# A table of expert products stored in blocks of two experts by two tokens instead of row by row

## The chip, the cores and the metric

The kernel runs on one core of a Trainium2 chip. The metric is the device time of one execution in microseconds (us); the time before is the median of three runs. A core has a matrix engine (PE, whose weight loads are listed as PEld), a vector engine (DVE), an activation engine (ACT), a general engine (POOL) and a queue engine (SP), which run side by side, each through its own instructions in order, and wait for each other by semaphores. Matrix products land in PSUM, all other tiles lie in SBUF; both have 128 partitions.

## The reference

The reference is one layer of a streaming encoder on 256 tokens of width 2048: a mixing block (gated MLP and retention) and then PEER, a lookup into 16384 experts. The change is in PEER. Expert number `n1 * 128 + n2` has a row of `emb_u` and a row of `emb_v`. For each token, 8 heads pick 16 experts each, 128 picks in all:

```python
    q = (hf @ wq).reshape(t_, PEER_HEADS, 2, PEER_DHALF)
    sc = jnp.einsum('thpd,hpnd->thpn', q, subkeys)
    v1, i1 = lax.top_k(sc[:, :, 0], PEER_TOPK)
    v2, i2 = lax.top_k(sc[:, :, 1], PEER_TOPK)
    cand = (v1[..., :, None] + v2[..., None, :]).reshape(t_, PEER_HEADS, ...)
    cidx = (i1[..., :, None] * PEER_NKEYS + i2[..., None, :]).reshape(...)
    top, sel = lax.top_k(cand, PEER_TOPK)
    eidx = jnp.take_along_axis(cidx, sel, axis=-1)
    gate = jax.nn.softmax(top, axis=-1)
    u = emb_u[it]
    a = jnp.einsum('td,thkd->thk', xt, u)
    w = jax.nn.gelu(a, approximate=False) * gt
    vv = emb_v[it]
    return jnp.einsum('thk,thkd->td', w, vv)
```

## The kernel before, in words

The kernel computes the PEER sums mostly as dense products over all experts, and only a slice of the columns by gathering rows. It goes through these stages:

- up to about 1119 us, the mixing block, the queries and the routing (`route_post`), which leaves for each token and pick the two halves `i1`, `i2` of the expert's number and the gate;
- 1119 to 1600 us, the u-products. For each value `n` of `i1`, PE multiplies the 128 experts of that block (columns 768 to 2047 of `emb_u`) with all 256 tokens. The results of two values of `i1` come to one PSUM bank, and line 926 copies it into `A`. `A` has 128 partitions (the `i2` of an expert) and 128 x 256 floats in each: by `i1`, then by token. It is 128 KB a partition. The other 768 columns are done by gathered rows (line 757) and dot products on DVE (line 764);
- 1600 to 1806 us, pick and scatter. The tokens go through in 32 units of 8 (`SET`). `one_hot` writes for each token a 128x128 matrix that has a one where the column's number is the pick's `i2` (`o2`, lines 960 and 961 on ACT or 957 on DVE, some tokens on POOL at line 963) or its `i1` (`o1`). `turned` transposes `o2` on PE (line 974, PSUM tile `pb`) and copies the result on ACT (line 975, `oh2T`). `pick` (line 984) multiplies it with all 128 values of `A` that belong to one token, so that each of the token's 128 picks gets the row of its `i2` (PSUM tile `pk`); line 988 on DVE takes from that row the value at its `i1`. `weight` adds the gathered part and makes the weight of each pick with GELU and the gate (lines 993 to 995). `scatter` multiplies `o1` by the weights on POOL (line 1000), PE sums them by expert (line 1004, PSUM tile `pw`), and ACT writes the 128x128 weights of four tokens back over the products in `A` (line 1005, the *put*);
- 1808 to 2327 us, the v-products. For each value `i` of `i1`, `v_load` takes the row `A[:, i]` of 256 token weights, splits it in a rounded part `wh` (line 1085, ACT) and a rest `wl` (line 1087, DVE), splits a block of `emb_v` likewise (lines 1089 and 1091), and PE sums the three products over all 128 blocks (line 1141). Gathered rows of `emb_v` (line 757) are weighed and added on DVE (line 1073) four gathers late. The end adds the residual and normalises.

In `A` of before, the values of one token are 256 floats (1024 bytes) apart, the values of one `i1` lie side by side. So line 926 writes side by side, line 984 reads with steps of 1024 bytes, line 1005 writes with steps of 1024 bytes (it goes through its source in order, token by token), and lines 1085 and 1087 read side by side.

The order of the work is written out by loops: in iteration `u` of the stage come `pick(u)`, `weight(u)`, the one-hot and the transposes of unit `u + 1`, `scatter(u - 2)`, and the one-hot `o1` of unit `u`. A scheduler then fixes one order for each engine. The PSUM tiles have 2 (`pb`), 3 (`pk`) and 3 (`pw`) buffers, the one-hots 3 (`o1`) and 5 (`o2`), the turned ones 4.

Of the kernel before, what the change touches and what calls it, by code (L numbers as in the profile page):

```python
# [10 lines left out]
F32 = mybir.dt.float32  # L11
# [5 lines left out]
ALU = mybir.AluOpType  # L17
# [5 lines left out]
P = 128  # L23
T = 256
# [9 lines left out]
NK = 128  # L34
# [82 lines left out]
def block_kernel(ctx, tc, a, out):  # L117
    nc = tc.nc
    def pool(name, side, bufs=1, space=None):
        stack = ExitStack()  # L120
        kw = {} if space == bass.MemoryType.DRAM else {"reuse_waits": "tile"}
        if space is not None:
            kw["space"] = space
        return stack.enter_context(tc.tile_pool(name=name, bufs=bufs, side=side, **kw)), stack
# [642 lines left out]
    def dot(tt, n, early=False, after=None):  # L767
        if early:
            g = gather(late["pg"], "eg", u_rows, UG, EG, tt, n)
        else:  # L770
            g = gather(ph, "hT", u_rows, UG, 8, tt, n, after)
        times(g, tt, n)
# [102 lines left out]
    def columns():  # L875
        softmax()
        nc.scalar.copy(idr, ident)
        for dst, src in ((i1T, i12[:, 0]), (i2T, i12[:, 1]), (gT, gate)):
            pt = bank("pt")
            for tt in range(TT):  # L880
                nc.tensor.transpose(pt[:, tt * P:(tt + 1) * P], src[:, tt], ident)
            nc.scalar.copy(dst, pt[:, :T])
            if dst is i2T:
                nc.scalar.mul(neg, pt[:, :T], -1.0)
# [4 lines left out]
    sums = {}  # L889

    def u_products(n):
        for m in range(n + len(ready), min(n + 2, 2 * NK)):
            ready.append(u_load(m))
        hi, lo = ready.pop(0)
        first, last = n % 2 == 0, n % 2 == 1
        if n % 4 == 0:
            sums[n // 4] = bank("mmu").rearrange("p (b t) -> p b t", b=2) if n // 4 % 2 else pm.tile([P, 2, T], F32, tag="mm", name="mmu")
        acc = sums[n // 4][:, n // 2 % 2]
        k0, k1 = HALF[n % 2]
        steps = ((hi, 0), (hi, 1), (lo, 0)) if n >= DIRECT else ((hi, None),)  # L900
        for i, (w, part) in enumerate(steps):
            for k in range(k0, k1):
                x = late["x1T"][:, UK + k] if part is None else h2T.op(part, UK + k)
                mm = nc.tensor.matmul(acc, w[:, k - k0], x, start=(first and k == 0 and i == 0),  # L904
                                      stop=(last and k == FK - 1 and i == len(steps) - 1))
        return mm

    for n in range(DIRECT):
        mm = u_products(n)
    late["pg_s"].close()  # L910
    st_s.close()
    big, big_s = pool("big", "left")
    A = big.tile([P, NK, T], F32, tag="big", name="A")
    pick_room, pick_room_s = pool("pickroom", "left")
    colT = pick_room.tile([P, 4, T], F32, name="colT")
    i1T, i2T, wT, gT = (colT[:, i] for i in range(4))
# [5 lines left out]
    for n in range(2 * NK):  # L922
        if n >= DIRECT:
            mm = u_products(n)
        if n % 4 == 3:
            nc.scalar.copy(A[:, n // 2 - 1:n // 2 + 1], sums.pop(n // 4))
        if n == COLS:
            columns()
        while done < rate * (n + 1 - PRE):
            dot(*todo.pop(0), after=mm)  # L930
            done += 1
# [10 lines left out]
    def psum(tag, bufs):  # L942
        b = pq.tile([P, 512], F32, tag=tag, bufs=bufs, name=tag)
        return b, b.rearrange("p (t n) -> p t n", t=4)
# [33 lines left out]
    def pick(u):  # L978
        for h in range(2):
            t0 = u * SET + 4 * h  # L980
            oh = ohs.pop((u, h))
            pk, pkv = psum("pk", 3)
            for t in range(4):
                mm = nc.tensor.matmul(pkv[:, t], oh[:, t], A[:, :, t0 + t], start=True, stop=True)
                tc.declare_no_dep(mm.ins, group="scattered", reason="other tokens' columns")
            for t in range(4):
                jk = p2.tile([P, P], F32, tag="jk", bufs=2, name="jk")
                nc.vector.scalar_tensor_tensor(jk, iota, i1T[:, t0 + t:t0 + t + 1], pkv[:, t],
                                               op0=ALU.is_equal, op1=ALU.mult, accum_out=wT[:, t0 + t:t0 + t + 1])
# [7 lines left out]
    def scatter(u):  # L997
        t0 = u * SET
        o1, o2 = o1s.pop(u), o2s.pop(u)
        nc.gpsimd.tensor_tensor(o1, o1, wT[:, t0:t0 + SET, None].to_broadcast([P, SET, P]), op=ALU.mult)  # L1000
        for h in range(0, SET, 4):
            pw, pwv = psum("pw", 3)
            for t in range(4):
                nc.tensor.matmul(pwv[:, t], o2[:, h + t].bitcast(F32), o1[:, h + t], start=True, stop=True)  # L1004
            put = nc.scalar.copy(A[:, :, t0 + h:t0 + h + 4].rearrange("p n t -> p t n"), pwv)
            tc.add_to_no_dep_group("scattered", put.ins)

    units = T // SET
# [18 lines left out]
    for u in range(-LEAD, units + LAG):  # L1027
        if 0 <= u < units and u % half == 0:
            tt = u // half
            while tt and fetched:  # L1030
                last_dot()
            pt, _ = psum("pk", 3)
            nc.tensor.transpose(pt[:, :P], wrow[:, tt], ident)
            nc.vector.tensor_copy(agT[:, tt * P:(tt + 1) * P], pt[:, :P])
        if 0 <= u < units:
            pick(u)
            weight(u)
        if u + LEAD < units:
            o2s[u + LEAD] = one_hot(1, u + LEAD, (ON2 if u * SET < T // 2 else ON3)[u % 4])
            turned(u + LEAD)  # L1040
        if 0 <= u < half and fetched and (u + 1) * LEFT > took * half:
            last_dot()
        if u >= LAG:
            scatter(u - LAG)
        if 0 <= u + 1 - LAG + AHEAD1 < units:
            v = u + 1 - LAG + AHEAD1
            o1s[v] = one_hot(0, v, ON1[v % 4])
        if 0 <= u < units and u % half == half - 1:
            pt, _ = psum("pk", 3)
            nc.tensor.transpose(pt[:, :P], wT[:, tt * P:(tt + 1) * P], ident)  # L1050
            nc.vector.tensor_copy(wrow[:, tt], pt[:, :P])
    W = A

    p2_s.close()
    pq_s.close()
    pick_room_s.close()
# [23 lines left out]
    def v_load(i):  # L1080
        room, bufs = (p3, 1) if i % 3 == 2 else (pv, 2)
        vb = room.tile([P, GV], F32, tag="vb", bufs=bufs, name="vb")
        nc.sync.dma_start(vb, v_cols[i * P:(i + 1) * P])
        wh = p3.tile([P, T], F32R, tag="wh", bufs=3, name="wh")
        nc.scalar.copy(wh, W[:, i])  # L1085
        wl = p3.tile([P, T], F32R, tag="wl", bufs=3, name="wl")
        nc.vector.tensor_tensor(wl, W[:, i], wh.bitcast(F32), op=ALU.subtract)  # L1087
        vh = p3.tile([P, GV], F32R, tag="vh", bufs=2, name="vh")
        nc.scalar.copy(vh, vb)  # L1089
        vl = p3.tile([P, GV], F32R, tag="vl", bufs=2, name="vl")  # L1090
        late["split"] = nc.vector.tensor_tensor(vl, vb, vh.bitcast(F32), op=ALU.subtract)  # L1091
        return vh, vl, wh, wl

    spent = A.rearrange("p n t -> p (n t)")
    x1 = spent[:, :TT * D].rearrange("p (t d) -> p t d", t=TT)
    xo = spent[:, TT * D:2 * TT * D].rearrange("p (t d) -> p t d", t=TT)
    ga2, gf = spent[:, 4 * D:5 * D], spent[:, 5 * D:6 * D]
# [39 lines left out]
    def product(i, ops, j, tt, n):  # L1137
        vh, vl, wh, wl = ops
        l, r = ((wh, vh), (wl, vh), (wh, vl))[j]
        c, w = chunks[n]  # L1140
        return nc.tensor.matmul(yp[tt][n][:, :w], l[:, tt * P:(tt + 1) * P], r[:, c:c + w],  # L1141
                                start=(i == 0 and j == 0), stop=(i == NK - 1 and j == 2))

    nxt = v_load(0)
    nc.scalar.sqrt(rf, late["ssum"])  # L1145
    done, rate = 0, len(todo) / (NK - ENDS)
    for i in range(NK - 2):
        ops = nxt
        nxt = v_load(i + 1)
        for j in range(3):  # L1150
            for tt in range(TT):
                for n in range(len(chunks)):
                    mm = product(i, ops, j, tt, n)
        while todo and done < rate * (i + 1):
            fly(*todo.pop(0), after=mm)
            done += 1
        while len(flying) > BEHIND:
            weigh()
        if i == BACK:
            restore(mm)  # L1160
    ends = [nxt, v_load(NK - 1)]
    while flying:
        weigh()
# [64 lines left out]
```

## Time and profile before

| what | value |
| --- | --- |
| median of three runs | 2359.65 us (2357.73, 2359.65, 2369.08) |
| the profiled execution | 2363.87 us |
| its span, first to last instruction | 2362.1 us |
| PE busy | 2199.1 us, 93% |
| DVE busy | 1779.2 us, 75% |
| ACT busy | 1028.9 us, 44% |
| POOL busy | 938.0 us, 40% |
| mean granted clock of PE | 0.978 |

Busy time is that of the whole span; the stages have different limits, and the shares of one stage are read from windows. A busy PE is one that has products under way, which overlap; the time from the start of one group of products to the start of the next tells what a group takes.

### The profile page before, as it was taken

Reading aid. Unit: us, or ns where it says so; the run is one execution under the profiler, and the core shown is the slowest. Engines: PE = TensorE matmul, PEld = TensorE weight load, DVE = VectorE, ACT = ScalarE, POOL = GpSimd, SP = SyncE. Lnnn points to the kernel's source line nnn. Section 1 sums busy time; section 2 is a strip of 40 time slices with the busy share of each in tenths; the row PEclk is TensorE's granted clock in tenths of the full one; section 3 lists DMA queues with packets and bytes.
Section 4 is the critical chain, followed back from the end, with each engine's and each line's share of the span. In section 5 each row is a group of like instructions: output and inputs, shape, how many; then the busy total and the mean of one; then the engine's idle time right before and its main releaser. Section 6 shows DMA issues by size and latency. Waiting matters only on the chain. (4 is left out here: it accounts for less than half of the span.)

```text
span 2362.1 us, 37306 instructions
## 1 busy us (share of the span) xinstructions
PE 2199.1 (93%) x13988; PEld 1953.3 (83%) x13988; DVE 1779.2 (75%) x3416; ACT 1028.9 (44%) x1439; POOL 938.0 (40%) x750
## 2 busy tenths in 40 slices
PE   6899999999999998983999999998999999999996
PEld 3577778999999888883899899898998878778885
DVE  3469878888888755788677767668766878888887
ACT  3245555643344344100344444447875444344433
POOL 0000000000000001766344444348776887887884
PEclk9999999999999999996999999999999999999998
DMA  9987778778877864767899899893103999999997
GB/s 352 370 308 270 276 276 290 267 285 291 289 280 291 286 209 166 275 203 228 292 307 312 303 309 312 294 310 102 54 1 112 327 331 318 323 333 331 340 323 265
DMA packets 144313, 638.27 MB, mean 270 GB/s; under 512 B 20721, under 2 KB 26625, under 8 KB 112001
## 3 DMA queue, kind: packets, MB, share of 16 engines
q1 hardware_dynamic: 102146, 459.65, 54.7%
q0 software_dynamic: 41984, 176.23, 21.7%
q8 instruction: 110, 1.80, 0.3%
q14 instruction: 73, 0.60, 0.1%
HBM read 631.59 MB, written 4.20 MB: 269 GB/s over the span
## 5 line engine op out<-in xcount | busy, mean ns | idle before, releaser
L757 POOL DMA_INDIRECT gat<-in_peer_v_rows,eidx x256 | 417.3, 1630 | 106.6 <-issue 40.2
L757 POOL DMA_INDIRECT gat<-in_peer_u_rows,eidx x256 | 313.0, 1223 | 309.8 <-DVE ulo L712 149.1
L213 ACT CAST whi<-wt 128x2048 fp32r<-128x2048 f32 x130 | 248.1, 1908 | 290.7 <-PE mm L414 222.8
L764 DVE SCALAR_TENSOR_TENSOR gat<-gat,h2b 128x768 f32<-128x768 f32 x256 | 245.2, 960 | 151.0 <-DMA gat<-in_peer_u_rows,eidx 147.9
L904 PE MATMUL mmu<-h2T,uhi 128*128 128x256 f32 x2360 | 325.8, 285 | 33.9 <-ACT uhi L711 33.9
L215 DVE TENSOR_TENSOR wlo<-wt,whi 128x2048 fp32r<-128x2048 f32 (+1 forms) x130 | 292.3, 2249 | 54.9 <-ACT whi L213 51.0
L904 PEld LDWEIGHTS mmu<-h2T,uhi 128*128 128x128 f32 x2360 | 303.8, 194 | 34.9 <-ACT uhi L711 34.8
L358 POOL DMA_DIRECT2D br<-in_b_ada x32 | 15.8, 493 | 771.3 <-DVE ada_acc L359 724.9
L1089 ACT CAST vh<-vb 128x1472 fp32r<-128x1472 f32 x128 | 183.0, 1430 | 303.9 <-DMA vb<-in_peer_v_cols 205.4
L711 ACT CAST uhi<-ub 128x640 fp32r<-128x640 f32 x236 | 171.3, 728 | 275.2 <-DMA ub<-in_peer_u_cols 216.3
L1073 DVE SCALAR_TENSOR_TENSOR yg<-gat,wrow,yg 128x576 f32<-128x576 f32 x254 | 207.9, 819 | 77.6 <-DMA gat<-in_peer_v_rows,eidx 71.5
L355 DVE SCALAR_TENSOR_TENSOR ada_acc<-wa,sc_col,ada_acc 128x256 f32<-128x256 f32 x480 | 231.7, 483 | 11.4
L1091 DVE TENSOR_TENSOR vl<-vb,vh 128x1472 fp32r<-128x1472 f32 x128 | 215.7, 1685 | 11.4 <-ACT vh L1089 11.3
L904 PE MATMUL mmu<-h2T,ulo 128*128 128x256 f32 x1180 | 189.4, 291 | 34.4 <-DVE ulo L712 33.5
L1141 PE MATMUL yp<-vl,wh 128*128 128x512 f32 (+1 forms) x768 | 195.4, 388 | 14.1 <-DVE vl L1091 12.2
L904 PEld LDWEIGHTS mmu<-h2T,ulo 128*128 128x128 f32 x1180 | 159.2, 193 | 48.5 <-DVE ulo L712 47.5
L1141 PE MATMUL yp<-vh,wh 128*128 128x512 f32 (+1 forms) x768 | 193.1, 385 | 4.6 <-ACT wh L1085 2.6
L712 DVE TENSOR_TENSOR ulo<-ub,uhi 128x640 fp32r<-128x640 f32 x236 | 188.7, 820 | 4.6 <-ACT uhi L711 4.3
L1141 PE MATMUL yp<-vh,wl 128*128 128x512 f32 (+1 forms) x768 | 191.7, 383 | 0.2 <-DVE wl L1087 0.2
L1141 PEld LDWEIGHTS yp<-vl,wh 128*128 128x128 f32 x768 | 142.1, 188 | 48.9 <-DVE vl L1091 20.6
L414 PE MATMUL mm<-whi,hT 128*128 128x512 f32 (+1 forms) x832 | 181.7, 362 | 0.0
L1141 PEld LDWEIGHTS yp<-vh,wh 128*128 128x128 f32 x768 | 145.2, 190 | 31.4 <-ACT vh L1089 3.0
(274 smaller groups left out, 3689.4 us busy)
## 6 DMA issues: line engine op xcount, KB each, us to landing
wa<-in_w_ada SPq DMA_DIRECT2D x96, 1024.0 KB
vb<-in_peer_v_cols SPq DMA_DIRECT2D x128, 736.0 KB
ub<-in_peer_u_cols SPq DMA_DIRECT2D x256, 320.0 KB
wt<-in_w_vg SPq DMA_DIRECT2D x32, 1024.0 KB
wt<-in_w_branch_gate SPq DMA_DIRECT2D x32, 1024.0 KB
wt<-in_w_u SPq DMA_DIRECT2D x16, 1024.0 KB
wt<-in_w_b_out SPq DMA_DIRECT2D x16, 1024.0 KB
wt<-in_w_o SPq DMA_DIRECT2D x16, 1024.0 KB
```

The lines of the kernel that those rows point to most:

```text
L213: nc.scalar.copy(hi, wt)
L215: nc.vector.tensor_tensor(lo[:, :cut], wt[:, :cut], hi[:, :cut].bitcast(F32), op=ALU.subtract)
L355: nc.vector.scalar_tensor_tensor(acc, wt[:, k], s, acc, op0=ALU.mult, op1=ALU.add)
L414: nc.tensor.matmul(job.ps[b], l, r, start=(first and k == 0 and i == 0 and not lo_part), stop=(last and k == job.rows - 1 and lo_part == 1))
L712: (nc.gpsimd if n < POOL else nc.vector).tensor_tensor(lo[:, :w], ub[:, :w], hi[:, :w].bitcast(F32), op=ALU.subtract)
L757: d = nc.gpsimd.indirect_dma_start(out=g, out_offset=None, in_=table, in_offset=bass.IndirectOffsetOnAxis(ap=rows_of("idx")[:, tt, n:n + 1 ...
L764: nc.vector.scalar_tensor_tensor(g, g, 1.0, h2b[:, tt, :UG], op0=ALU.mult, op1=ALU.mult, accum_out=pe["wrow"][:, tt, n:n + 1])
L904: mm = nc.tensor.matmul(acc, w[:, k - k0], x, start=(first and k == 0 and i == 0), stop=(last and k == FK - 1 and i == len(steps) - 1))
L1073: d = nc.vector.scalar_tensor_tensor(yg[:, tt], g, w, yg[:, tt], op0=ALU.mult, op1=ALU.add)
L1089: nc.scalar.copy(vh, vb)
L1091: late["split"] = nc.vector.tensor_tensor(vl, vb, vh.bitcast(F32), op=ALU.subtract)
L1141: return nc.tensor.matmul(yp[tt][n][:, :w], l[:, tt * P:(tt + 1) * P], r[:, c:c + w], start=(i == 0 and j == 0), stop=(i == NK - 1 and j = ...
```

## The change

`A` gets five dimensions in place of three: 64 pairs of `i1`, 128 pairs of tokens, and in each such block two values of `i1` by two tokens. The four floats of a block lie side by side (16 bytes), first the two tokens of the first `i1`, then those of the second. The size is the same. All reads and writes of `A` follow:

- the copy after the u-products (line 926 before, 932 after) writes 512 floats side by side and goes through its PSUM source two tokens at a time, in turn from one `i1` and the other;
- the pick (984, 990 after) reads for one token two floats 8 bytes apart, then jumps 2048 bytes to the next pair of `i1`;
- the put (1005, 1012 after) writes for four tokens runs of 8 floats (two blocks, 32 bytes), 2048 bytes apart, and reads PSUM in that order: two tokens that lie 512 bytes apart in turn, then the next `i1`;
- `wh` and `wl` (1085 and 1087, 1091 and 1093 after) read two floats side by side and jump 16 bytes from pair to pair; what they write stays side by side.

Every engine has the same instructions in the same order with the same waits as before; only the operands' steps differ.

```diff
-    A = big.tile([P, NK, T], F32, tag="big", name="A")
+    A = big.tile([P, NK // 2, T // 2, 2, 2], F32, tag="big", name="A")
+
+    def of_key(n):
+        return A[:, n // 2, :, n % 2, :]
+
+    def of_token(t):
+        return A[:, :, t // 2, :, t % 2]
...
-            nc.scalar.copy(A[:, n // 2 - 1:n // 2 + 1], sums.pop(n // 4))
+            nc.scalar.copy(A[:, n // 4], sums.pop(n // 4).rearrange("p b (g s) -> p g b s", s=2))
...
-                mm = nc.tensor.matmul(pkv[:, t], oh[:, t], A[:, :, t0 + t], start=True, stop=True)
+                mm = nc.tensor.matmul(pkv[:, t].rearrange("p (m b) -> p m b", b=2), oh[:, t], of_token(t0 + t), start=True, stop=True)
...
-            put = nc.scalar.copy(A[:, :, t0 + h:t0 + h + 4].rearrange("p n t -> p t n"), pwv)
+            g0 = (t0 + h) // 2
+            put = nc.scalar.copy(A[:, :, g0:g0 + 2], pwv.rearrange("p (g s) (m b) -> p m g b s", s=2, b=2))
...
-    W = A
-
...
-        nc.scalar.copy(wh, W[:, i])
+        w = of_key(i)
+        nc.scalar.copy(wh.rearrange("p (g s) -> p g s", s=2), w)
...
-        nc.vector.tensor_tensor(wl, W[:, i], wh.bitcast(F32), op=ALU.subtract)
+        nc.vector.tensor_tensor(wl.rearrange("p (g s) -> p g s", s=2), w, wh.bitcast(F32).rearrange("p (g s) -> p g s", s=2), op=ALU.subtract)
...
-    spent = A.rearrange("p n t -> p (n t)")
+    spent = A.rearrange("p m g b s -> p (m g b s)")
```

## Rows read from the trace of the kernel before

**Rows 1.** The page's slices: busy tenths of each engine in 40 equal parts.
```profile
span 2362.1 us, 37306 instructions
...
PE   6899999999999998983999999998999999999996
...
DVE  3469878888888755788677767668766878888887
ACT  3245555643344344100344444447875444344433
POOL 0000000000000001766344444348776887887884
PEclk9999999999999999996999999999999999999998
DMA  9987778778877864767899899893103999999997
```

**Rows 2.** Windows over five stretches: busy us and instructions of each engine.
```profile
core 0: us, PE busy (x) PEld busy (x) DVE busy (x) ACT busy (x) POOL busy (x), PEclk, DMA share, GB/s
1119.00:1600.00 481.00, 447.70 (x3537) 433.01 (x3537) 338.04 (x586) 200.91 (x302) 206.69 (x174) 0.99 0.90 303
1602.00:1611.00 9.00, 5.07 (x24) 4.59 (x25) 7.84 (x14) 6.45 (x17) 8.15 (x6) 0.54 0.59 182
1615.00:1705.00 90.00, 88.59 (x588) 84.48 (x587) 69.47 (x310) 70.97 (x152) 67.99 (x60) 1.00 0.19 56
1711.21:1794.71 83.50, 83.50 (x558) 80.00 (x556) 57.29 (x272) 62.48 (x128) 65.70 (x66) 1.00 0.00 1
1808.00:2327.00 519.00, 505.22 (x2250) 420.86 (x2251) 433.46 (x502) 219.71 (x256) 416.75 (x256) 1.00 0.92 326
```

**Rows 3.** Timeline of PE: the picks of units 1 and 16.
```profile
1612.52 3.86 PE L984 MATMUL pk<-A,oh2T 128*128 128x128 f32 x16 [0.17 <-ACT oh2T L975]
...
1706.57 3.67 PE L984 MATMUL pk<-A,oh2T 128*128 128x128 f32 x16
```

**Rows 4.** Timeline of PE: one unit of the second half (start us, us).
```profile
1780.14 0.99 PE L974 MATMUL pb<-idr,oh 128*128 128x128 f32 x8
1780.96 2.02 PE L1004 MATMUL pw<-oh 128*128 128x128 f32 x16
1782.82 3.67 PE L984 MATMUL pk<-A,oh2T 128*128 128x128 f32 x16
1786.14 1.00 PE L974 MATMUL pb<-idr,oh 128*128 128x128 f32 x8
```

**Rows 5.** Waits in 1600 to 1810: us in total, times, longest.
```profile
ACT oh2T L975 <- PE pb L974: 30.5, 27, 2.7
DVE jk L988 <- PE pk L984: 29.8, 51, 1.8
POOL oh L963 <- PE pw L1004: 27.1, 23, 2.0
ACT A L1005 <- PE pw L1004: 16.3, 21, 3.3
```

**Rows 6.** Groups by form in 1600 to 1810, ACT: busy us, mean ns.
```profile
L1005 ACT COPY A<-pw 128x512 f32<-128x512 f32 x64 | 64.2, 1049 | 16.5 <-PE pw L1004 16.3 <-issue 0.2
...
L975 ACT COPY oh2T<-pb 128x512 f32<-128x512 f32 x64 | 34.6, 590 | 31.0 <-PE pb L974 30.5 <-issue 0.5
```

**Rows 7.** Line 926 alone: duration in ns, minimum, median and maximum.
```profile
L926 ACT COPY A<-mmu x64: 576/580/632, 1119.7 to 1599.6; 128x512 f32<-128x512 f32 x64
```

**Rows 8.** Lines 1085 and 1087 alone, in the same form.
```profile
L1085 ACT CAST wh<-A x128: 387/398/408, 1807.9 to 2327.5; 128x256 fp32r<-128x256 f32 x128
...
L1087 DVE TENSOR_TENSOR wl<-A,wh x128: 406/418/476, 1809.6 to 2331.3; 128x256 fp32r<-128x256 f32 x128
```

## The prediction

> **What bounds the kernel now.** I read the slices of the span first: TensorE (PE) is at 8 or 9 tenths nearly everywhere, but in slices 28 to 31 (some 1600 to 1830 us) the DMA share drops to 3, 1, 0 and 3 tenths, so there the kernel lives on its engines alone [rows 1]. That is the pick and scatter stage, the only one where `A` is read by token. Windows over the stages come next [rows 2]. [...] In the first half (1615 to 1705, at 6.27 us a unit, from 1612.52 and 1706.57, the starts of the picks of units 1 and 16: 94.05 / 15 [rows 3]) PE is busy 88.59 of 90 us, ACT 70.97, DVE 69.47, POOL 67.99: per unit, times 6.27 / 90, ACT 4.94, DVE 4.84, POOL 4.74. [...] PE's timeline splits the unit [rows 4]: from 1780.14 transposes 0.82 us, scatter products 1.86 (1780.96 to 1782.82), pick products 3.32 (1782.82 to 1786.14), together 6.00. The pick and scatter products have the same shape and count, 16 records of 128x128 f32 each (two for one product), and last 2.02 and 3.67 us. They differ in the moving operand: scatter's `o1` is read element by element, pick's `A[:, :, t]` in steps of T floats, 1024 bytes. Waits confirm who is late: DVE's 29.8 us for `pk`, ACT's 30.5 for `pb`, POOL's 27.1 and ACT's 16.3 for `pw` all end on PE [rows 5].
>
> The stages on both sides matter less: in 1808 to 2327 PE is at 505.22 of 519 us, DVE 433.46, ACT 219.71, DMA share 0.92; in 1119 to 1600 PE is at 447.70 of 481, DMA 0.90 [rows 2].
>
> **The change part by part.** No instruction is added, removed or moved, and no wait is: only the steps of four operations' operands differ.
>
> *Pick (L984), 256 products.* A token's 128 values now lie in pairs: two floats 8 bytes apart inside 16 bytes, then a jump of 2048 bytes. Bounds: as now, 3.32 us a unit, gain nothing; as contiguous, 1.86 us, gain 3.32 - 1.86 = 1.46, or by durations 3.67 - 2.02 = 1.65. The slowdown now is a factor 1.8 in the step from one float to the next when each lies far from the last. With two in 16 bytes far jumps are halved, so if one jump costs about what two near reads cost (what 3.32 against 1.86 suggests), the pairs hide it. I take the contiguous price with a gain of 1.55: PE falls from 5.96 to 4.4 us a unit. [...]
>
> *Put (L1005), 64 copies.* Now it reads PSUM in order and writes with steps of 1024 bytes: 1049 ns, against 590 for the copy L975 of the same 128x512 from PSUM to a packed tile [rows 6]. After, it writes runs of 8 floats (32 bytes) and reads PSUM with a step of 512 bytes at nearly every element. The scatter has moved from the writing side to the reading side. Bounds: 590 if PSUM is read as fast in steps, and, nothing in the trace reading PSUM so, above 1049 without a row to stop it; the nearest row for one far jump per element is 1049 itself. I take 1049. The difference of the lower bound, 2 x 0.46 = 0.92 us of ACT a unit, is a rival below. [...]
>
> *Filling A (L926), 64 copies at 580 ns* [rows 7]. Reads pairs from PSUM, writes packed. Bounds 580 and 1049: at worst 64 x 0.47 = 30 us of ACT in a stage of 481 us where ACT has 280 idle [rows 2]. Hidden: nothing.
>
> *Splits of a key's row (L1085 on ACT, 398 ns; L1087 on DVE, 418 ns), 128 each* [rows 8]. They read two floats, then jump 16 bytes: near jumps only. Bounds: as now; or ACT's 0.92 ns an element more from the put ((1049 - 580) / 512), 256 x 0.92 = 0.23 us each. DVE's 433.46 us of 519 would become 463 (0.23 x 128 = 30), still under PE; what covers it is DVE's own slack. I take nothing, and 5 us at worst, where `vl` comes later than PE's queue is long.
>
> *The sum.* PE's saving is 32 x 1.55 = 50 us if nothing else held. But the next engines do. First half: ACT at 4.94 becomes the bound, with DVE 4.84 and POOL 4.74 close behind. ACT's work is also lumpy: three one-hots in four are made there. Today the stage loses 6.27 - 6.00 = 0.27 a unit with the next engine 1 us below; with three engines within 0.2 us, I choose twice that, 0.5: 5.45 us, 15 x (6.27 - 5.45) = 12 us. Second half: POOL 4.69 plus 0.4 (PE at 4.4 and ACT at 4.46 below it) = 5.1: 14 x (5.96 - 5.1) = 12 us. The three units at the ends, where PE waits for one-hots anyway (busy 5.07 of 9 us at 1602 to 1611 [rows 2]), I give 1 us together. Sum 25 us. The stage after starts 25 us earlier and runs as before: its first loads already wait in place, since the DMA share in 1711 to 1794 is 0.00.
>
> The profiled execution is 2363.87 us (span 2362.1, so 1.8 outside it); it lies 4.2 above the median of 2359.65. From 2363.87 the sum gives 2339; from the median, which I forecast, 2335.
>
> **The rivals.**
>
> *The put becomes short as well.* For it: the write is packed, and L975 costs 590. Against: its reads jump. Then ACT falls by 0.92 to 4.02 and 3.54; DVE 4.84 bounds the first half, POOL 4.69 the second. With 0.3 of stall: 5.14 and 4.99; 15 x 1.13 + 14 x 0.97 + 2 = 33 us: 2327. With no stall at all 15 x 1.43 + 14 x 1.27 + 2 = 41: 2319, the lower bound.
>
> *The picks stay slow.* Then PE stays the limit at 5.96 and nothing else in the stage matters while ACT stays under it: 2359. For it: every pair still begins with a far jump. Against: the factor is 1.8, not more.
>
> *The put becomes longer (the slower side).* ACT's cost a unit is 4.94 + 2(p - 1.049) and 4.46 + 2(p - 1.049) for a put of p us. It reaches today's 6.27 at p = 1.71 in the first half and 5.96 at p = 1.80 in the second: from there the change loses. Between 1.3 and 1.7 most of the gain is eaten. At p = 2.1, with both a far read and a slow one, ACT needs 7.04 and 6.56: 15 x 0.77 + 14 x 0.60 = 20 us slower, 2380. For it: PSUM is read out of order 512 times a copy, 64 copies. Against: the far writes of today cost only a factor 1.8.
>
> [...]
>
> **How the numbers follow.** Put unchanged and picks fast (the forecast, 2335): 0.45. Put short: 0.28. Picks stay slow: 0.10. Put between 1.3 and 1.7: 0.10. Put longer than that or another loss: 0.07. A change under 0.5% (12 us, 2348 to 2371) is about what a measurement here can't tell from none. Faster takes the first two and 0.04 of the fourth, 0.77; same the third and the rest of the fourth, 0.16; slower 0.07. The range runs from the lower bound to the half-eaten gain: 2318 to 2352. It holds the first two cases and part of the fourth.
>
> **What would show it.** Sixteen pick records in about 2.0 us where they took 3.67; the mean of the put near 1049; the stage from the first pick to the first product of the last stage shorter by 25 us; DVE's wait for `pk` much smaller; waits in the stage that end on ACT and POOL in place of PE, among them PE for `oh2T` and `oh`. The means of L926, L1085 and L1087 within 5% of 580, 398 and 418. The prediction is wrong if the picks still take over 3 us a unit, if the put is over 1.3 us, or if the last stage takes more than 5 us longer than its 519.

## The result and the profile after

The changed kernel takes 2332.88 us (median of four runs, 2331.0 to 2334.47) against 2359.16 of the kernel before beside it: ratio 0.9887, 95% interval 0.9868 to 0.9906, so 26.3 us or 1.1% faster. The profiled execution took 2331.0 us with a span of 2329.2.

The time is read in two stretches: the pick stage, from the first pick product on PE to the first v-product, and the v-products, from their first to their last start.

| stretch, us | before | after |
| --- | --- | --- |
| first pick to first v-product | 1605.01 to 1808.36: 203.35 | 1604.01 to 1779.52: 175.5 |
| first to last v-product | 535.3 | 529.5 |

The pick stage gives 27.9 us. The 5.8 of the v-products can't be put down to the change: four kernels below that alter nothing in that stage (e1, e2, r1 and r2) lie anywhere from 525 to 533 us in it. The profiled execution of before is also 4.7 above its median here; against the median the pick stage alone accounts for the gain.

The windows of after over the five stretches that answer to [rows 2], moved to where the stages now lie (busy us and instructions of each engine):

```profile
core 0: us, PE busy (x) PEld busy (x) DVE busy (x) ACT busy (x) POOL busy (x), PEclk, DMA share, GB/s
1119.00:1600.00 481.00, 444.06 (x3537) 429.86 (x3537) 339.97 (x589) 201.45 (x306) 210.60 (x177) 0.99 0.91 304
1601.00:1610.00 9.00, 5.26 (x29) 4.83 (x29) 8.36 (x16) 6.44 (x17) 8.14 (x7) 0.62 0.55 172
1614.00:1693.00 79.00, 66.68 (x565) 64.46 (x566) 72.32 (x302) 59.80 (x150) 70.52 (x59) 0.96 0.22 62
1699.01:1767.77 68.76, 62.14 (x558) 60.19 (x557) 66.25 (x264) 51.93 (x127) 68.15 (x66) 1.00 0.01 2
1779.50:2299.00 519.50, 508.93 (x2263) 425.62 (x2264) 435.32 (x505) 221.96 (x254) 406.98 (x256) 0.99 0.93 328
```

In the second half of the pick stage PE, which was busy all the time, is at 62.14 of 68.76 us; POOL is now at 68.15 (99%) and DVE at 66.25 (96%). In the first half DVE is at 92%, POOL at 89%, PE at 84%, ACT at 76%. The bound has moved from PE to DVE and POOL together, not to ACT. The stages on both sides look as before.

The lines that the change touches, each alone (duration in ns: minimum, median, maximum), which answer to [rows 6 to 8]:

```profile
L932 ACT COPY A<-mmu x64: 574/580/628, 1120.8 to 1598.5; 128x512 f32<-128x512 f32 x64
...
L990 PE MATMUL pk<-A,oh2T x512: 270/272/582, 1604.0 to 1769.5; 128*128 128x128 f32 x171
...
L1012 ACT COPY A<-pw x64: 567/586/613, 1622.2 to 1777.2; 128x512 f32<-128x512 f32 x64
...
L1091 ACT CAST wh<-A x128: 407/418/433, 1779.0 to 2299.2; 128x256 fp32r<-128x256 f32 x128
...
L1093 DVE TENSOR_TENSOR wl<-A,wh x128: 408/417/425, 1780.8 to 2301.0; 128x256 fp32r<-128x256 f32 x128
```

The pick is short, and so is the put: 586 ns where it took 1049. `wh` is 20 ns longer, `wl` and the fill are unchanged. PE's timeline, first a stretch at the start of the stage, then a unit of the second half, answers to [rows 3, 4]:

```profile
1616.85 0.88 PE L980 MATMUL pb<-idr,oh 128*128 128x128 f32 x8
1620.13 3.65 PE L1010 MATMUL pw<-oh 128*128 128x128 f32 x16 [2.40 <-POOL oh L1006]
1623.61 1.95 PE L990 MATMUL pk<-A,oh2T 128*128 128x128 f32 x16
...
1743.00 2.05 PE L990 MATMUL pk<-A,oh2T 128*128 128x128 f32 x16 [0.56 <-ACT oh2T L981]
1744.81 0.88 PE L980 MATMUL pb<-idr,oh 128*128 128x128 f32 x8
1745.53 2.02 PE L1010 MATMUL pw<-oh 128*128 128x128 f32 x16
1748.12 2.06 PE L990 MATMUL pk<-A,oh2T 128*128 128x128 f32 x16 [0.57 <-ACT oh2T L981]
```

Sixteen pick records last 1.95 to 2.06 us (3.67 before), and PE now stands before them. At 1620.13, behind a wait of 2.40 us, the scatter's sixteen records took 3.65 us in place of 2.02; the granted clock in 1620 to 1624 is 0.57, where it is 1.00 in 1612 to 1620 and in 1624 to 1656. The waits of the stage, which answer to [rows 5] (us in total, times, longest):

```profile
ACT colT L1000 <- DVE colT L999: 20.3, 20, 2.2
ACT A L1012 <- PE pw L1010: 15.0, 26, 2.9
...
PE pw L1010 <- POOL oh L1006: 10.2, 9, 2.4
ACT oh2T L981 <- PE pb L980: 8.8, 10, 1.9
...
PE pb L980 <- ACT oh L967: 6.3, 4, 3.7
PE pk L990 <- ACT oh2T L981: 6.2, 10, 1.5
...
DVE jk L994 <- PE pk L990: 4.0, 4, 1.7
```

DVE's wait for `pk` fell from 29.8 us to 4.0. PE waits for POOL's scaled one-hots and for ACT; and ACT waits 20.3 us for the weights' first step on DVE (L999), which cost it 1.4 us in before. DVE itself has become slower. The groups by form (busy us, mean ns), in 1600 to 1810 of before, then in 1600 to 1785 of after, and behind them DVE and POOL of after in a stretch of the second half:

```profile
L957 DVE TENSOR_TENSOR oh<-kst,colT 128x896 f32<-128x896 f32 x32 | 36.0, 1127 | 6.7 <-PE pw L1004 6.7
...
L993 DVE TENSOR_TENSOR colT<-colT,agT 128x8 f32<-128x8 f32 x32 | 7.7, 240 | 0.3
```

```profile
L963 DVE TENSOR_TENSOR oh<-kst,colT 128x896 f32<-128x896 f32 x32 | 43.6, 1366 | 3.5 <-PE pw L1010 3.5
...
L999 DVE TENSOR_TENSOR colT<-colT,agT 128x8 f32<-128x8 f32 x32 | 14.9, 466 | 0.3
```

```profile
1706.17 1.89 POOL L1006 TENSOR_TENSOR oh<-oh,colT 128x1024 f32<-128x1024 f32 x1
1706.36 2.65 DVE L963 TENSOR_TENSOR oh<-kst,colT 128x896 f32<-128x896 f32 x1
1708.93 0.15 DVE L999 TENSOR_TENSOR colT<-colT,agT 128x8 f32<-128x8 f32 x1
1709.01 1.18 DVE L963 TENSOR_TENSOR oh<-kst,colT 128x896 f32<-128x896 f32 x1
```

The one-hot of seven tokens takes 1.08 us at the least, 1.18 here beside POOL's own one-hots, and 2.65 when POOL's product is under way: it ends at 1709.01, 0.95 us after the product. Its mean is 1366 ns against 1127 in before (there line 957), that of L999 466 against 240 (there line 993). The one-hot of seven tokens, L999 and POOL's product have two SBUF inputs each; what holds the one up behind the other, the rows don't show.

### The profile page after: what moved, and what is told of

The parts are those of the page before. It is cut to its first block, busy times and chain, and to the rows that moved or that the text cites. A ratio compares the mean times of both kernels' runs of the same rounds, so it can differ in the third digit from the quotient of the medians.

```text
span 2329.2 us, 37299 instructions
## 1 busy us (share of the span) xinstructions
PE 2149.4 (92%) x13988; PEld 1909.8 (82%) x13988; DVE 1793.5 (77%) x3416; ACT 1008.0 (43%) x1439; POOL 936.7 (40%) x750
## 5 line engine op out<-in xcount | busy, mean ns | idle before, releaser
L757 POOL DMA_INDIRECT gat<-in_peer_v_rows,eidx x256 | 407.0, 1590 | 116.7 <-PE yp L1147 40.9
```

Source lines behind the costliest of these rows:

```text
L757: d = nc.gpsimd.indirect_dma_start(out=g, out_offset=None, in_=table, in_offset=bass.IndirectOffsetOnAxis(ap=rows_of("idx")[:, tt, n:n + 1 ...
```

## The experiments

Each ran beside the kernel before. "Stage" and "v" are the two stretches of the first table, in the profiled execution; of after they are 175.5 and 529.5.

| kernel | us | ratio, 95% interval | stage | v |
| --- | --- | --- | --- | --- |
| after | 2332.88 | 0.9887 (0.9868 to 0.9906) | 175.5 | 529.5 |
| e1, put alone | 2355.51 | 0.9988 (0.9967 to 1.0009) | 200.5 | 530.2 |
| e2, picks alone | 2331.61 | 0.9893 (0.9846 to 0.994) | 177.9 | 525.3 |
| e3, two by four | 2356.8 | 0.9991 (0.9973 to 1.0009) | 200.8 | 525.4 |
| e4, four by one | 2312.3 | 0.9813 (0.9777 to 0.9849) | 176.4 | 510.4 |
| f1, wl in steps | 2313.39 | 0.9809 (0.9784 to 0.9835) | 176.4 | 510.2 |
| f2, wh in steps | 2333.01 | 0.9887 (0.9863 to 0.9912) | 176.3 | 524.4 |
| r1, less on POOL | 2328.33 | 0.9862 (0.982 to 0.9903) | 169.5 | 533.3 |
| r2, least on POOL | 2317.93 | 0.9827 (0.9798 to 0.9856) | 160.5 | 530.6 |
| g1, a gap behind wl | 2316.9 | 0.9816 (0.9793 to 0.984) | 176.7 | 511.3 |
| c2, before, wl in steps | 2356.05 | 0.9984 (0.9967 to 1.0001) | 203.1 | 527.5 |
| c3, f1 and r2 together | 2297.87 | 0.974 (0.9715 to 0.9764) | 160.4 | 511.9 |
| c4, before, a gap | 2341.57 | 0.9935 (0.9911 to 0.9959) | 203.5 | 510.4 |

### Picks and put taken apart

**e1** is the kernel before with the put's elements in another order: it writes four tokens side by side and reads PSUM at steps of 512 bytes.

```diff
-            put = nc.scalar.copy(A[:, :, t0 + h:t0 + h + 4].rearrange("p n t -> p t n"), pwv)
+            put = nc.scalar.copy(A[:, :, t0 + h:t0 + h + 4], pwv.rearrange("p t n -> p n t"))
```

> The old layout; only the put goes through the four tokens first, so that it writes 16 bytes side by side and reads PSUM in steps of 512 bytes. Theory (PE alone set the pace of the stage, and the picks are what was shortened): the put falls to about 590 ns as in the changed kernel, the picks stay at 3.67 us a unit, a unit stays at 5.9 to 6.0 us, and the time stays at 2354 to 2362. Rival (the put's 0.92 us of ACT a unit was what the stage gained by): half or more of the 26 us comes here, 2346 or less.

```profile
L984 PE MATMUL pk<-A,oh2T 128*128 128x128 f32 x512 | 118.4, 397 | 1.2 <-ACT oh2T L975 1.2
...
L1005 ACT COPY A<-pw 128x512 f32<-128x512 f32 x64 | 37.4, 586 | 24.9 <-PE pw L1004 24.8
```

The put fell to 586 ns, the picks stayed at 397 ns a record, and the time can't be told from that of before. The stage is 200.5 us where before, c2 and c4, with the old put, take 203.1 to 203.5: while PE is the limit, the put is worth some 2.7 us and no more.

**e2** is the changed kernel with the put in an order that writes with far steps again.

```diff
-            put = nc.scalar.copy(A[:, :, g0:g0 + 2], pwv.rearrange("p (g s) (m b) -> p m g b s", s=2, b=2))
+            put = nc.scalar.copy(A[:, :, g0:g0 + 2].rearrange("p m g b s -> p b g s m"), pwv.rearrange("p (g s) (m b) -> p b g s m", s=2, b=2))
```

> The new layout; only the put goes through its elements with the pair of experts innermost, so that each write is 2048 bytes from the last, as far apart as before the change. Theory (after the change DVE and POOL set the pace, ACT has 1 us a unit to spare): the put returns to about 1049 ns, the picks stay at 1.95 us a unit, and the time is 2332 to 2338. Rival (with a put of 1049 ns ACT sets the pace, as the prediction had it): ACT above 95% busy in the first half, a unit there at 5.8 us or more, and 2340 to 2346.

The put was 1056 ns, as the prediction had assumed, and yet the stage lost only 2.4 us to after. Its windows in the two halves:

```profile
1612.00:1692.00 80.00, 67.52 (x565) 65.11 (x565) 74.16 (x310) 69.20 (x148) 71.24 (x60) 0.94 0.22 61
1700.00:1765.00 65.00, 59.23 (x521) 57.60 (x521) 63.30 (x252) 57.74 (x122) 64.11 (x62) 0.97 0.01 2
```

In the first half ACT is at 69.20 of 80 us, below POOL with 71.24 and DVE with 74.16; in the second POOL and DVE are at 99% and 97%. So ACT doesn't bind even with the long put, and the picks alone make nearly all of the gain: 25.4 of the 27.9 us of the stage, and 2331.61 us in all.

**e3** asks whether it is nearness that helps the picks, or the same 16 bytes: blocks of two values of `i1` by four tokens, so that a token's two values lie 16 bytes apart.

```diff
-    A = big.tile([P, NK // 2, T // 2, 2, 2], F32, tag="big", name="A")
+    A = big.tile([P, NK // 2, T // 4, 2, 4], F32, tag="big", name="A")
...
-        return A[:, :, t // 2, :, t % 2]
+        return A[:, :, t // 4, :, t % 4]
...
```

> Blocks of two experts by four tokens, so that a token's two values lie 16 bytes apart in place of 8; put, fill and splits stay packed or nearly so. Theory (what counts is that both values lie in the same 16 bytes): the picks are back at 3.67 us a unit, the put stays at 590 ns, and the time is 2354 to 2362. Rival (it is the long jump that costs, and a step of 16 bytes is a near one): picks at 1.95 to 2.1 us a unit and 2331 to 2336.

```profile
L990 PE MATMUL pk<-A,oh2T 128*128 128x128 f32 x512 | 118.4, 397 | 1.3 <-ACT oh2T L981 1.3
```

The picks are back at 397 ns a record, the put stays at 587, and the gain is gone but for what e1 has too. Values 16 bytes apart are as slow as values 1024 apart (397 ns in both kernels); with two in the same 16 bytes, in after, a pick record takes 272 ns in the median, and one of the scatter, read element by element, 275.

**e4** goes the other way: four values of `i1` of one token in a block, and the values of one `i1` 16 bytes apart for `wh` and `wl` (shown against the changed kernel).

```diff
-    A = big.tile([P, NK // 2, T // 2, 2, 2], F32, tag="big", name="A")
+    A = big.tile([P, NK // 4, T, 4], F32, tag="big", name="A")
...
-        return A[:, n // 2, :, n % 2, :]
+        return A[:, n // 4, :, n % 4]
...
-        return A[:, :, t // 2, :, t % 2]
+        return A[:, :, t]
...
```

> Blocks of four experts by one token: a pick reads four values side by side, but a row of 256 weights is now read at steps of 16 bytes by the splits. Theory (a value alone in its 16 bytes costs ACT and DVE as much more as it cost the put, 0.92 ns each): wh and wl take about 0.23 us more each, 0.65 us, DVE goes from 435 to about 465 us busy in the v-products' 519, and that stage hides most of it: 2331 to 2340. Rival (that stage has no room on DVE): the v-products take 15 us longer or more and the time is 2346 or more. Second rival (reads of ACT and DVE don't care for the step): wh and wl within 5% of 418 ns, 2331 to 2336.

Picks and put are about as in after (in the mean 289 ns a record for 280, and 585 for 586): four values in the same 16 bytes make a pick no faster than two. `wh` rose to 650 ns and `wl` to 612, near the 0.65 us that was expected of one value in 16 bytes. But the v-products, which have more work on ACT and DVE now, became 19 us *shorter*. No theory had that sign, and the next runs went after it.

### Why slower splits made the v-products faster

**f1** and **f2** are the changed kernel with one of the two reads of `A` alone in steps of 16 bytes (first all even tokens, then all odd ones; `wh` and `wl` themselves are then gone through in steps of 8 bytes).

```diff
-        nc.vector.tensor_tensor(wl.rearrange("p (g s) -> p g s", s=2), w, wh.bitcast(F32).rearrange("p (g s) -> p g s", s=2), op=ALU.subtract)
+        nc.vector.tensor_tensor(wl.rearrange("p (g s) -> p s g", s=2), w.rearrange("p g s -> p s g"), wh.bitcast(F32).rearrange("p (g s) -> p s g", s=2), op=ALU.subtract)
```

> The changed kernel; only the subtraction that makes wl (DVE) goes through its elements with the pairs of tokens outermost, so that it reads the table at steps of 16 bytes, as in the blocks of four by one, while the cast that makes wh stays as it is. Theory (in the blocks of four by one the v-products gained 19 us because wl's way of reading lets POOL's gathers through between DVE's instructions): wl takes about 0.61 us, a gather on POOL falls from 1.6 to about 1.3 us, first to last v-product takes 508 to 516 us and the time is 2309 to 2320. Rival (it came from wh, or from the picks' layout): 2329 to 2340, since DVE only gets 25 us more to do.

```diff
-        nc.scalar.copy(wh.rearrange("p (g s) -> p g s", s=2), w)
+        nc.scalar.copy(wh.rearrange("p (g s) -> p s g", s=2), w.rearrange("p g s -> p s g"))
```

> The counterpart: only the cast that makes wh (ACT) reads the table at steps of 16 bytes, and wl stays as it is. Theory (wl made the gain): wh takes about 0.65 us, gathers on POOL stay at 1.6 us, first to last v-product takes 524 to 532 us, the time is 2328 to 2337. Rival (a longer wh shifts wl behind the gathers): 508 to 516 us and 2309 to 2320.

A `wl` of 616 ns brings the 19 us, a `wh` of 654 ns brings nothing. With the slow `wl` a gather on POOL takes 1307 ns in the mean, in after 1593. DVE and POOL in the v-products of after:

```profile
2073.00 0.42 DVE L1093 TENSOR_TENSOR wl<-A,wh 128x256 fp32r<-128x256 f32 x1
2073.34 0.81 DVE L1078 SCALAR_TENSOR_TENSOR yg<-gat,wrow,yg 128x576 f32<-128x576 f32 x1
2073.49 3.09 POOL L757 DMA_INDIRECT gat<-in_peer_v_rows,eidx  x1 [0.30 <-DVE wl L1093]
2074.07 1.68 DVE L1097 TENSOR_TENSOR vl<-vb,vh 128x1472 fp32r<-128x1472 f32 x1
2075.67 0.81 DVE L1078 SCALAR_TENSOR_TENSOR yg<-gat,wrow,yg 128x576 f32<-128x576 f32 x1
```

The gather comes 0.15 us after DVE has gone on to `yg`, and takes 3.09 us: it waits out `yg` and `vl`, which ends at 2075.75, and is through 0.83 us later, although the next `yg` is under way by then. The whole stretch shows it: of 197 gathers in 1850 to 2250 of after, 130 take over 1.1 us, and each of these ends 0.82 us (0.815 to 0.831) after some instruction of DVE does; behind 107 of them DVE's next one has already begun. So a held gather waits here for the end of one or two instructions of DVE, not for a pause. Of the gathers, 39 come 0.1 to 0.2 us after a `yg` that stands behind `wl`; they take 2.39 us in the mean. In f1 the gather comes ahead of `yg`:

```profile
2074.42 0.95 POOL L757 DMA_INDIRECT gat<-in_peer_v_rows,eidx  x1 [0.30 <-issue]
...
2074.47 0.80 DVE L1078 SCALAR_TENSOR_TENSOR yg<-gat,wrow,yg 128x576 f32<-128x576 f32 x1
```

**g1** tests that it is the time between `wl` and `yg` that counts, not how `wl` reads. It is the changed kernel with a small instruction on DVE with one SBUF input, queued right behind `wl`; its result goes unused.

```diff
...
+        with tc.high_priority():
+            gap = nc.vector.tensor_reduce(p3.tile([P, 1], F32, tag="gap", bufs=2, name="gap"), iota, axis=AX.X, op=ALU.max)
+        tc.add_manual_dep(gap.ins, wlo.ins.name, QUEUED, reason="right behind it")
```

> The changed kernel, with wl read as it is there, and one more instruction on DVE right behind each wl, which takes the maximum over 128 constants (its result is not used; one operand in SBUF, some 0.2 us). Theory (what counts is the time from the start of wl to DVE's next instruction with two SBUF operands: a gather comes to POOL's turn 0.48 us after wl's start, DVE goes on after 0.34 us in the changed kernel and after 0.5 us where wl reads in steps): DVE goes on after about 0.54 us, gathers fall from 1.6 to about 1.3 us, first to last v-product takes 508 to 517 us, and the time is 2309 to 2321 although DVE has 25 us more to do. Rival (it is the steps in wl's reading that let POOL through): gathers at 1.6 us, 524 to 535 us, 2330 to 2342.

```profile
2073.43 0.42 DVE L1093 TENSOR_TENSOR wl<-A,wh 128x256 fp32r<-128x256 f32 x1
2073.77 0.28 DVE L1095 TENSOR_REDUCE gap<-kst 128x1 f32<-128x128 f32 x1
2073.91 0.95 POOL L757 DMA_INDIRECT gat<-in_peer_v_rows,eidx  x1 [0.30 <-DVE wl L1093]
2073.97 0.80 DVE L1078 SCALAR_TENSOR_TENSOR yg<-gat,wrow,yg 128x576 f32<-128x576 f32 x1
2074.69 1.68 DVE L1100 TENSOR_TENSOR vl<-vb,vh 128x1472 fp32r<-128x1472 f32 x1
```

The gather starts 0.06 us before `yg` and is through in 0.95, and so are all 50 that start within 0.1 us ahead of a `yg` behind the gap. The v-products take 511.3 us. So 0.28 us of added work on a busy DVE, 128 times, takes 16 us off the kernel's time (18 off the v-products of the profiled execution): the gathers come back sooner (in 1850 to 2250, 1285 ns in the mean in place of 1593), `yg` waits less for them (29.1 us in place of 58.5), PE waits less for `vl` (1.2 in place of 9.8), and PE is busy 398.77 of 400 us in place of 389.45. The gap has one SBUF input, and the gather that starts while it runs (2073.91, the gap to 2074.05) isn't held by it; that 0.15 us decide it comes from these rows.

**c2** and **c4** try the two edits on the kernel before. With four tokens in 16 bytes there, c2 also reads `wh` and writes `wl` in steps of 16 bytes, where f1 has steps of 8.

```diff
-        nc.vector.tensor_tensor(wl, W[:, i], wh.bitcast(F32), op=ALU.subtract)
+        nc.vector.tensor_tensor(wl.rearrange("p (g s) -> p s g", s=4), W[:, i].rearrange("p (g s) -> p s g", s=4), wh.bitcast(F32).rearrange("p (g s) -> p s g", s=4), op=ALU.subtract)
```

> The kernel before, with its table row by row; only wl goes through a row in steps of four tokens, 16 bytes. Theory (what the steps bring has nothing to do with the picks): wl at about 0.61 us, first to last v-product 508 to 517 us where the kernel before takes 525 to 536, picks at 3.67 us a unit, and 2334 to 2345. Rival (it needs the stage of the picks to be short): 2352 to 2362.

> The kernel before, with its own layout, and on DVE an instruction of some 0.28 us with one SBUF input (over the constant row of numbers) queued right behind wl in every v-load; in the changed kernel the same instruction shortened the v-products from 529.5 to 511.3 us. Theory that the time between wl and the next two-operand instruction is all that a gather needs to get in: it does the same here, v-products from 535.3 to 514 to 518, gathers near 1300 ns, 2337 to 2343 us. Rival that in this layout the gathers run too late in their queue for it, as the run with steps in wl alone suggested: v-products 524 to 532, gathers still over 1500 ns, 2350 to 2360 us.

The gap works there too: 2341.57 us, with v-products of 510.4 and gathers of 1301 ns. So the gap has nothing to do with the layout. The slow `wl` doesn't work in c2, though it lasts 627 ns:

```profile
1949.95 0.64 DVE L1087 TENSOR_TENSOR wl<-A,wh 128x256 fp32r<-128x256 f32 x1
1950.43 1.70 POOL L757 DMA_INDIRECT gat<-in_peer_v_rows,eidx  x1 [0.30 <-issue]
1950.50 0.80 DVE L1073 SCALAR_TENSOR_TENSOR yg<-gat,wrow,yg 128x576 f32<-128x576 f32 x1
...
2072.06 0.63 DVE L1087 TENSOR_TENSOR wl<-A,wh 128x256 fp32r<-128x256 f32 x1
2072.53 0.97 POOL L757 DMA_INDIRECT gat<-in_peer_v_rows,eidx  x1 [0.30 <-issue]
2072.60 0.80 DVE L1073 SCALAR_TENSOR_TENSOR yg<-gat,wrow,yg 128x576 f32<-128x576 f32 x1
```

Both gathers come 0.07 us ahead of `yg`; one gets in, the other waits `yg` out. Of the 47 that come within 0.1 us ahead of a `yg` behind `wl` (1850 to 2250), 27 are through in 1.1 us and 20 take 1.69 to 4.58; in f1 all 48 of that kind take 0.95 at most. The mean of a gather is still 1579 ns. So coming first is not enough in every case. Whether it is the farther steps of `wh` and `wl` in c2 that keep the gather out is open; no run separates them.

### Who bounds the pick stage now

**r1** and **r2** are the changed kernel with fewer of the one-hot tokens on POOL (its share of eight tokens, for `o1` and `o2`, in each half of the stage); DVE and ACT make them instead.

```diff
-SHARE1, SHARE2 = (1, 1), (1, 3)
+SHARE1, SHARE2 = (1, 1), (1, 2)
```

> The changed kernel; in the second half of the picks POOL makes two of eight one-hots of i2 in place of three, the engine that makes the others (ACT in three units of four, DVE in one) makes six. Theory (POOL and DVE set the pace of a unit at 4.9 us, both over 96% busy, and ACT has 1 us to spare): POOL's busy time falls by 0.6 us a unit, a unit of the second half takes 4.6 to 4.8 us, the time from the first pick to the first v-product falls from 175.5 to 170 to 174 us. Rival (PE's waits for the turned one-hots of ACT set it): 176 to 182 us.

```diff
-SHARE1, SHARE2 = (1, 1), (1, 3)
+SHARE1, SHARE2 = (0, 1), (0, 2)
```

> The changed kernel; POOL makes no one-hot of i1 any more (DVE makes all eight), and in the second half two of i2 in place of three. Theory (DVE waits behind POOL, more than the one-hots cost it): POOL's busy time falls by 0.9 us a unit in the first half and 1.5 in the second, DVE's instructions with two SBUF operands get shorter (its one-hot of i1 from 1.37 to 1.25 us although it makes one more), the time from the first pick to the first v-product is 165 to 172 us. Rival (DVE is the bound by its own work and now has 0.15 us more a unit): 175 to 182 us.

The stage takes 169.5 us in r1 and 160.5 in r2; that is 15 less than in after, and a larger gain than was expected. r2's windows:

```profile
1612.00:1692.00 80.00, 68.40 (x614) 66.22 (x612) 76.28 (x324) 66.18 (x167) 67.88 (x46) 1.00 0.26 78
1700.00:1760.00 60.00, 59.08 (x547) 58.67 (x545) 55.86 (x266) 51.63 (x128) 52.57 (x38) 1.00 0.01 2
```

In the second half PE is the bound again, at 59.08 of 60 us, and a unit takes 4.27 us (picks at 1736.39 and 1740.66); in the first half DVE still is, at 76.28 of 80. DVE took over one token more in each `o1` and yet lasts no longer: 1337 ns for eight against 1366 for seven (1250 was expected), since POOL holds it up less: at the least eight take 1.21 us and seven 1.08, so the hold has shrunk from 0.29 to 0.13 us in the mean. In the 14 units from 17 to 31 DVE's busy time fell from 66.25 to 57.49 us. The move was worth more than the instructions that it took off POOL.

**c3** joins r2 and f1.

> The changed kernel with both: wl in steps of 16 bytes, and POOL with the fewest one-hots (none of i1, two of i2 in the second half). Theory (the two gains lie in two stages and add): first pick to first v-product 159 to 163 us, first to last v-product 508 to 514 us, 2294 to 2304. Rival (the earlier start of the v-products collides with something else): 2306 or more.

2297.87 us, 2.6% under before: the gains add, 160.4 and 511.9 us. It is the fastest of all.

## Why the prediction was right, and where it wasn't

The forecast was 2335 us in a range of 2318 to 2352; 2332.88 was measured. The sum came out at 25 us for the stage and 27.9 were seen. That it came so close is in part luck: the first half gave 10.0 us (15 x (6.27 - 5.60)) where 12 were taken, the second 14.8 (14 x (5.97 - 4.91)) where 12 were, the ends 3.0 where 1 was, and behind the two halves stand a put that was priced too high and an overlap of DVE and POOL that was not counted. PE's 5.96 us a unit of the second half, POOL's 4.69 and ACT's 4.46, from which the sum starts, are a fourteenth of the fourth window of [rows 2]: it runs over 14 units, from the picks of unit 17 to those of unit 31, and PE is busy in all of it.

- **Picks.** Right. A unit's picks take 1.70 us from start to start (r2's unhindered PE) in place of 3.32: 1.62 gained where 1.55 was taken. The transposes take 0.72 there in place of 0.82, so PE needs 4.28 us a unit, not 4.4. e3 (397 ns a record, 272 in after) shows that it is the shared 16 bytes.
- **Put.** This is the term that was mis-sized: taken unchanged at 1049 ns by the argument that the far steps only change sides, measured at 586. With PSUM read in steps of 512 bytes the ACT copy takes 586 ns, in order (L981) 583, and the lower bound from L975 was the true row.
- **Who is next.** "ACT at 4.94 becomes the bound" in the first half failed. With the put at its true price ACT is at 76%, and e2 shows that even at 1056 ns it would not have been the bound. The put is worth 1 to 2.4 us (e2's stage of 177.9 against 175.5 to 176.7 in the kernels with the picks and POOL's share of after and a short put), not the 8 that lay between the forecast and the rival, and the time of e2 doesn't show it.
- **The stall.** The rival with the short put, whose ACT was right, gave 5.14 and 4.99 us a unit; 5.60 ((1694.86 - 1610.83) / 15, the picks of units 1 and 16) and 4.91 ((1767.77 - 1699.01) / 14, units 17 and 31) were measured. The missing 0.46 in the first half is 7 us. Neither case counted that DVE's and POOL's instructions get longer with PE out of the way (DVE's one-hot of `i1` from 1127 to 1366 ns, POOL's one-hots of `i2` from 707 to 841); the busy times of before hold the old overlap. DVE is busy 76.68 us in these 15 units, 5.11 a unit in place of 4.84: that is 0.27 of the 0.46, some 4 us. The rest, 0.19 a unit or 3 us, is stall beyond the 0.3 that was taken; what part of it the clock has is not shown.
- **PE's clock.** Sixteen records of scatter took 3.65 us for 2.02 behind PE's wait of 2.40, at the granted clock of 0.57; behind another wait, of 1.74 up to 1660.97, eight transposes took 1.22 us for 0.88 and twelve records of scatter 2.75, at 0.63 in 1660 to 1664. In sum that is some 3 us of PE's time, an estimate from these rows. The granted clock of the first half is 0.96 where it was 1.00 before. How much of the 3 us the stage lost, with PE no longer its bound, isn't shown.
- **Fill and splits.** Right: 580, 418 and 417 ns; only `wh` is at the edge of the 5% that were allowed.
- **The ends** gave 3.0 us, not 1: from the first pick to that of unit 1 6.82 us in place of 7.51, from unit 16 to 17 4.15 in place of 4.66, and from the last unit's picks (at 1767.77; at 1794.82 before) to the first v-product 11.75 in place of 13.54.
- **The last stage** runs as before, as was said. That it could be 19 us shorter without any change of layout was in no step.

## What to carry to other kernels

This table, written one way and read another, needed its two nearest partners inside the same 16 bytes, not all of them: in blocks of two by two a pick record takes 272 ns and `wh` and `wl` 418 and 417, where row by row the picks take 397 (`wh` 398, `wl` 418) and in blocks of four by one `wh` takes 650 and `wl` 612. When the bound goes, work out the next one from what the engines do to each other, not from busy times alone; moving work off POOL paid twice in r2, where DVE's busy time in 14 units also fell, from 66.25 to 57.49 us. And look at which of two engines comes first to each turn: a gap of 0.28 us in DVE's run was worth 16 us here and 15 in the kernel before, though c2 shows that coming first does not always get a gather in.

## What was not expected of the hardware

- One value per 16 bytes cost about the same nearly everywhere in these runs: (1049 - 586) / 512 = 0.90 ns an element for ACT's writes, (650 - 418) / 256 = 0.91 for its reads, (397 - 272) / 128 = 0.98 for PE's moving operand, (612 - 417) / 256 = 0.76 for DVE's reads. Two values per 16 bytes cost 0.08 on ACT's read ((418 - 398) / 256), and nothing that shows for PE (272 ns a pick record, 275 a scatter record) and for DVE's reads (417 for `wl`, 418 in before).
- ACT's put read PSUM at 512-byte steps about as fast as L981, of the same size, read it in order (586 against 583 ns).
- A gather on POOL took 0.95 us where nothing held it. Each of the 130 longer ones in 1850 to 2250 of after ends 0.82 us after a `vl` (92 of them), a `yg` (36) or a `wl` (2) of DVE does, all instructions with two SBUF inputs, though the next may have begun: 3.09 us behind `yg` and `vl`.
